# The first row tile in two column halves, one on ScalarE's DMA queue and one on SyncE's

## Chip, cores, metric

One core of a Trainium2 chip. The metric is the device time of one execution in microseconds (us), and medians of several executions are quoted. All runs used here are fast, with a mean granted TensorE clock of 0.64 to 0.67. Engines: PE (matmul), DVE (VectorE), ACT (ScalarE), POOL (GpSimd), SP (SyncE).

## The reference

```python
def reference(a, b):            # a, b: float32, 8 x 2176 x 2176
    prod = np.matmul(a, b)
    return np.diagonal(prod, axis1=1, axis2=2).sum(axis=-1).astype(np.float32)
```

The trace of a product is the sum of a[i,k] b[k,i]. So no matrix product is needed: each element of a and b is read once, multiplied with one partner and added. The inputs are 303 MB.

## The kernel before

For each of eight batches, row tiles of a are loaded, transposed on PE into `at`, and then row tiles of b are multiplied with it and summed, mostly on DVE. GpSimd issues nearly all loads and casts f32 to bf16 in the DMA. Two row groups of 512 rows go together in one load (4352 KB in SBUF), into one of three staging buffers:

```python
    stage = ctx.enter_context(tc.tile_pool(name="stage", bufs=3))
    single = ctx.enter_context(tc.tile_pool(name="single", bufs=3))
    ...
    def load(src, start, m, count):
        ...
        with in_order():
            issued = nc.gpsimd.dma_start(out=part, in_=rows)
```

The very first row tile (128 rows, 1.114 MB) is an exception. SyncE loads it as plain f32 into a staging buffer (`words`), and ACT and DVE cast half of it each:

```python
    def load_first(src, start):
        words = stage.tile([P, DOUBLE * ROWS, N], bf16, tag="stage")
        plain = words.bitcast(f32).rearrange("p r k -> p (r k)")[:, :N]
        half = N // 2
        t = single.tile([P, 1, N], bf16, tag="single")
        nc.sync.dma_start(out=plain, in_=src[start:start + P, :])
        nc.scalar.copy(out=t[:, 0, :half], in_=plain[:, :half])
        nc.vector.tensor_copy(out=t[:, 0, half:], in_=plain[:, half:])
        return [(start, 1, t)]
    ...
            if not tiles:
                groups = load_first(a[bi], start)
                ahead, issued = load(a[bi], *loads[1])
                with tc.issue_after(issued.ins):
                    constants()
            elif ahead is not None:
                groups, ahead = ahead, None
            else:
                groups, _ = load(a[bi], start, m, count)
```

`words` takes one of the three staging buffers, so GpSimd's third large load can be issued only after both casts. The first two large loads take the other buffers.

Of the kernel before, what the change touches and what calls it, by code (L numbers as in the profile page):

```python
# [20 lines left out]
def kernel(  # L21
# [6 lines left out]
    nc = tc.nc  # L28
    P = 128
# [58 lines left out]
    def load_first(src, start):  # L88

        words = stage.tile([P, DOUBLE * ROWS, N], bf16, tag="stage")  # L90
        plain = words.bitcast(f32).rearrange("p r k -> p (r k)")[:, :N]
        half = N // 2
        t = single.tile([P, 1, N], bf16, tag="single")
        nc.sync.dma_start(out=plain, in_=src[start:start + P, :])
        nc.scalar.copy(out=t[:, 0, :half], in_=plain[:, :half])  # L95
        nc.vector.tensor_copy(out=t[:, 0, half:], in_=plain[:, half:])  # L96
        return [(start, 1, t)]
# [119 lines left out]
    for bi in range(BATCH):  # L217
# [8 lines left out]
        for start, m, count in loads:  # L226
# [9 lines that stand above are left out]
            for start, m, a_t in groups:  # L236
                last_transpose = transpose_group(at, a_t, start, m, b_groups)
# [12 lines left out]
        for start, m, count in ([(*g, 1) for g in b_groups] if last else joined(b_groups)):  # L250
            if last and start == N - P:
# [3 lines left out]
                for g0, g1 in LAST_PIECES:  # L255
                    lo, hi = g0 * WIDE, min(g1 * WIDE, N)
                    with in_order():
                        loaded.append(nc.gpsimd.dma_start(  # L258
                            out=row[:, lo:hi], in_=b[bi, start:start + P, lo:hi]
# [3 lines left out]
                for g in range(2, n_wide):  # L263
                    half = ROWS // 2
# [21 lines left out]
            out=tiles["sums"][:, bi:bi + 1], in_=acc[:, :cols], axis=mybir.AxisListType.X  # L286
# [4 lines left out]
    with tc.issue_after(last_transpose.ins):  # L291
        for n, (x, y) in enumerate(pe_work):
            nc.tensor.matmul(  # L293
                trace_ps, x, y, start=(n == 0), stop=(n == len(pe_work) - 1),
            )
    late_acc = tiles["late"]
    for n, (x, y) in enumerate(late):
# [6 lines left out]
        start=True, stop=True,  # L304
    )
    parts = [tiles["sums"][:, BATCH - 1:BATCH]] + [late_acc[:, n:n + 1] for n in range(len(late) + 1)]
    for n, part in enumerate(parts):
        nc.tensor.matmul(  # L308
            total[:, BATCH - 1:BATCH], tiles["ones"], part,
            start=(n == 0), stop=(n == len(parts) - 1),  # L310
# [3 lines left out]
        out=out.rearrange("(a b) -> a b", a=1),  # L314
        in_=tiles["result"][:1, :BATCH],
# [31 lines left out]
```

## Time and profile before

| | before |
|---|---|
| time, median of the first 3 runs (range) | 710.42 us (710.14 to 710.47) |
| span of the profiled execution | 708.7 us |
| read from HBM | 303.04 MB, 428 GB/s over the span |
| first tile: issue, casts start | 0.74, 5.85 us |
| third large load issued | 7.25 us |
| first, second large load in use on PE | 26.40, 47.06 us |

The timeline's lines read: start, duration, engine, line, operation, output<-input, count, and in brackets the idle time before and who ended it. "ACTq" and "SPq" are DMA issues. The lines themselves stand in the prediction.

### The profile page before, as it was taken

What the parts mean: (1) busy time and instruction counts of PE and PEld (TensorE: products, weight loads), DVE (VectorE), ACT (ScalarE), POOL (GpSimd) and SP (SyncE); (2) the same over time, 40 slices, a digit from 0 to 9 for tenths busy, and PEclk for the clock granted to TensorE, in tenths of its full rate; (3) what the DMA queues carried; (4) which work ended last, traced back from release to release, by engine and by line L of the source; (5) the groups of instructions that cost most, each with busy time, mean ns of one, the idle gap of its engine ahead of it and who ended that gap; (6) DMA issues with size and microseconds to landing.
All of it is one profiled execution on the core that took longest, in us unless ns stands there. A gap on an engine that the chain in (4) does not pass through costs nothing.

```text
span 708.7 us, 3573 instructions
## 1 busy us (share of the span) xinstructions
PE 197.8 (28%) x1342; PEld 184.2 (26%) x1342; DVE 420.6 (59%) x455; ACT 196.8 (28%) x210; POOL 35.0 (5%) x61
## 2 busy tenths in 40 slices
PE   1542006420055100551006600056000670006705
PEld 0542005410054100550006500056000560005605
DVE  0223996139952399523994349943499334993396
ACT  2344005430064200652006510066000670006700
POOL 1000000000010000100001000000000000000010
PEclk9977556765577655776557765577655775557765
DMA  9999999999999999999999999999999999999997
GB/s 220 220 220 214 209 221 220 219 210 213 223 219 213 214 218 220 219 211 214 220 220 216 212 216 220 217 214 214 220 220 215 213 217 219 217 216 214 217 215 143
DMA packets 11635, 152.30 MB, mean 215 GB/s; under 512 B 866, under 2 KB 1122, under 8 KB 3298
## 3 DMA queue, kind: packets, MB, share of 16 engines
q0 software_dynamic: 11472, 150.97, 100.1%
q1 hardware_dynamic: 146, 1.11, 0.4%
q8 instruction: 10, 0.16, 0.1%
q14 instruction: 7, 0.06, 0.0%
HBM read 303.04 MB, written 0.00 MB: 428 GB/s over the span
## 4 chain that ended last, share of the span: by engine, by line
DMA 54%; DVE 29%; another core or an unknown queue 10%; PE 3%; issue 2%; ACT 1%; POOL 1%; DVEq 0%; POOLq 0%
DMA t<-in_b_dram 42%; DVE scratch L132 29%; DMA t<-in_a_dram 12%; PE ps L165 2%; ACT at L122 1%; POOL t L83 1%; PE trace_ps L293 0%; DVE acc L132 0%; DVEq L132 0%; PE ps L186 0%; POOL identity masks.py:199 0%; DVE at L120 0%; PE total L308 0%; POOL identity masks.py:197 0%
## 5 line engine op out<-in xcount | busy, mean ns | idle before, releaser
L132 DVE CUSTOM_DVE_ANT_1 scratch<-at,t 128x2048 bf16<-128x2048 bf16 (+1 forms) x159 | 319.6, 2010 | 76.7 <-DMA t<-in_b_dram 69.4
L122 ACT COPY at<-ps 128x1024 bf16<-128x1024 bf16 x208 | 194.5, 1039 | 472.0 <-PE ps L165 472.0
L165 PE MATMUL ps<-identity,t 128*128 128x128 f32 x1071 | 176.8, 332 | 480.5 <-DMA t<-in_a_dram 255.4
L165 PEld LDWEIGHTS ps<-identity,t 128*128 128x128 f32 x1071 | 164.9, 213 | 489.2 <-DVE sums L285 322.0
L120 DVE COPY at<-ps 128x1024 bf16<-128x1024 bf16 (+2 forms) x104 | 93.6, 903 | 201.0 <-PE ps L165 183.7
L83 POOL DMA_DIRECT2D t<-in_a_dram x23 | 15.4, 669 | 357.8 <-DVE acc L132 213.3
L83 POOL DMA_DIRECT2D t<-in_b_dram x27 | 17.0, 632 | 292.8 <-DVE acc L132 145.0
L186 PE MATMUL ps<-identity,t 128*128 128x128 bf16 x170 | 16.4, 219 | 5.3 <-DVE at L120 5.0
L293 PE MATMUL trace_ps<-t,at 128*128 128x128 bf16 x80 | 9.6, 290 | 22.7 <-DMA t<-in_b_dram 22.3
L293 PEld LDWEIGHTS <-at 128*128 128x128 bf16 x89 | 9.8, 122 | 23.6 <-issue 22.9
L186 PEld LDWEIGHTS <-t 128*128 128x128 bf16 x170 | 13.0, 100 | 8.5 <-issue 8.3
L132 DVE DVE_READ_ACCUMULATOR2_ANT acc<- 128x1 f32 x166 | 13.6, 82 | 0.0
L96 DVE CAST t<-words 128x1088 bf16<-128x1088 f32 x1 | 0.7, 727 | 5.0 <-DMA words<-in_a_dram 5.0
L132 DVE CUSTOM_DVE_ANT_1 scratch<-at,b_t 128x256 bf16<-128x256 bf16 (+1 forms) x3 | 1.5, 515 | 1.6 <-DMA b_t<-in_b_dram 1.6
L132 DVE CUSTOM_DVE_ANT_0 scratch<-at,t 128x128 bf16<-128x128 bf16 x7 | 2.0, 291 | 0.2
L95 ACT CAST t<-words 128x1088 bf16<-128x1088 f32 x1 | 1.1, 1098 | 3.8 <-DMA words<-in_a_dram 3.8
L258 POOL DMA_DIRECT2D b_t<-in_b_dram x3 | 1.6, 567 | 0.0
L285 DVE TENSOR_REDUCE sums<-acc 128x1 f32<-128x22 f32 (+1 forms) x8 | 1.4, 174 | 0.3
L95 ACT ACT_TABLE_LOAD x1 | 1.3, 1283 | 0.7 <-PEq L331 0.7
L293 PE MATMUL trace_ps<-b_t,at 128*128 128x128 bf16 x9 | 1.3, 290 | 0.0
L308 PE MATMUL total<-late,ones 128*1 128x1 f32 x8 | 0.5, 163 | 0.3 <-DVE late L132 0.3
masks.py:199 POOL TENSOR_SCALAR_AFFINE_SELECT identity<-identity 128x128 f32<-128x128 f32 (+1 forms) x2 | 0.5, 307 | 0.0
(14 smaller groups left out, 2.4 us busy)
## 6 DMA issues: line engine op xcount, KB each, us to landing
t<-in_a_dram POOLq DMA_DIRECT2D x16, 4352.0 KB, 44.1
t<-in_b_dram POOLq DMA_DIRECT2D x14, 4352.0 KB, 51.8
t<-in_b_dram POOLq DMA_DIRECT2D x3, 2176.0 KB, 32.4
t<-in_b_dram POOLq DMA_DIRECT2D x9, 544.0 KB, 54.8
t<-in_a_dram POOLq DMA_DIRECT2D x7, 544.0 KB, 45.5
words<-in_a_dram SPq DMA_DIRECT2D x1, 1088.0 KB, 5.1
t<-in_b_dram POOLq DMA_DIRECT2D x1, 1088.0 KB, 14.7
b_t<-in_b_dram POOLq DMA_DIRECT2D x1, 256.0 KB, 19.6
```

The lines of the kernel that those rows point to most:

```text
L83: issued = nc.gpsimd.dma_start(out=part, in_=rows)
L95: nc.scalar.copy(out=t[:, 0, :half], in_=plain[:, :half])
L96: nc.vector.tensor_copy(out=t[:, 0, half:], in_=plain[:, half:])
L120: last_copy = nc.vector.tensor_copy(out=dst, in_=src)
L122: nc.scalar.copy(out=dst, in_=src)
L132: nc.vector.tensor_tensor_reduce(out=out, in0=x, in1=y, scale=1.0, scalar=0.0, op0=MUL, op1=ADD, accum_out=acc,)
L165: nc.tensor.transpose(ps[:, n * m + r, :], words[:, r, c0:c0 + step * (P - 1) + 1:step], tiles[f32],)
L186: last_transpose = nc.tensor.transpose(ps16[:, n, r, :], a_t[:, r, c0:c0 + P], tiles[bf16],)
L258: loaded.append(nc.gpsimd.dma_start(out=row[:, lo:hi], in_=b[bi, start:start + P, lo:hi]))
L285: nc.vector.reduce_sum(out=tiles["sums"][:, bi:bi + 1], in_=acc[:, :cols], axis=mybir.AxisListType.X)
L293: nc.tensor.matmul(trace_ps, x, y, start=(n == 0), stop=(n == len(pe_work) - 1),)
L308: nc.tensor.matmul(total[:, BATCH - 1:BATCH], tiles["ones"], part, start=(n == 0), stop=(n == len(parts) - 1),)
```

## The change

Its intent: the two casts belong to two engines and need one half each. If each half is issued by a separate queue, both could be issued at once and ACT could start on its own half without waiting for the other.

```diff
-        nc.sync.dma_start(out=plain, in_=src[start:start + P, :])
+        nc.scalar.dma_start(out=plain[:, :half], in_=src[start:start + P, :half])
+        nc.sync.dma_start(out=plain[:, half:], in_=src[start:start + P, half:])
```

## The prediction

> **What bounds the kernel now**
>
> I read the page from the top: busy shares, the forty slices, the queues. Then the chain of waits, then the timeline of the first ten microseconds, and last the final twenty-five.
>
> Busy shares and slices first. No engine is near full, but the DMA row is full nearly everywhere.
>
> ```profile
> span 708.7 us, 3573 instructions
> PE 197.8 (28%) x1342; PEld 184.2 (26%) x1342; DVE 420.6 (59%) x455; ACT 196.8 (28%) x210; POOL 35.0 (5%) x61
> ...
> DMA  9999999999999999999999999999999999999997
> ...
> q0 software_dynamic: 11472, 150.97, 100.1%
> q1 hardware_dynamic: 146, 1.11, 0.4%
> ...
> HBM read 303.04 MB, written 0.00 MB: 428 GB/s over the span
> ```
>
> The reader is to see three things. The busiest engine (DVE) works 59% of the span. The software queue that GpSimd feeds, casting f32 to bf16 on the way (so 302 MB read become 151 MB written), takes 100% of the sixteen DMA engines' time. The hardware queue, on which the disputed first tile travels, takes 0.4%. So the kernel is bound by moving 303 MB; at 428 GB/s over the span, 1 MB read is worth 2.3 us, and the change neither adds nor removes a byte.
>
> Does the software queue ever run dry, so that an earlier release upstream could buy something? Where it feeds from:
>
> ```profile
> t<-in_a_dram POOLq DMA_DIRECT2D x16, 4352.0 KB, 44.1
> t<-in_b_dram POOLq DMA_DIRECT2D x14, 4352.0 KB, 51.8
> ...
> words<-in_a_dram SPq DMA_DIRECT2D x1, 1088.0 KB, 5.1
> ```
>
> A large load needs about 20.5 us of the engines (4.46 MB written at 217 GB/s; the first two land at 26.4 and 46.9 in the timeline, 20.5 apart), but stands 44 to 52 us between issue and landing. The difference, 23 us or more in the median, is time behind earlier loads. The thinnest place is the end: at 682.64 the loads of the last five row tiles begin to be issued, and the first of these lands 14.7 us later although its 1088 KB need 5.1 us; even there some 9.6 us of work is ahead in the queue.
>
> Now the start, where the change lies (timeline, 0 to 10 us: start, duration, engine, work, idle before it and who ended that):
>
> ```profile
> 0.74 1.28 ACT L95 ACT_TABLE_LOAD   x1 [0.74 <-PEq L331]
> 0.74 0.40 SPq L94 DMA_DIRECT2D words<-in_a_dram  x1
> 1.25 0.82 POOL L83 DMA_DIRECT2D t<-in_a_dram  x1 [0.80 <-POOLq L331]
> 2.93 0.72 POOL L83 DMA_DIRECT2D t<-in_a_dram  x1
> 5.85 1.10 ACT L95 CAST t<-words 128x1088 bf16<-128x1088 f32 x1 [3.83 <-DMA words<-in_a_dram]
> 5.85 0.73 DVE L96 CAST t<-words 128x1088 bf16<-128x1088 f32 x1 [4.98 <-DMA words<-in_a_dram]
> 7.06 1.58 PEld L165 LDWEIGHTS ps<-identity,t 128*128 128x128 f32 x8 [7.06 <-issue]
> 7.25 0.72 POOL L83 DMA_DIRECT2D t<-in_b_dram  x1 [3.60 <-ACT t L95]
> ...
> 26.40 6.39 PEld L165 LDWEIGHTS ps<-identity,t 128*128 128x128 f32 x32 [17.62 <-DMA t<-in_a_dram]
> ...
> 37.97 1.28 POOL L83 DMA_DIRECT2D t<-in_b_dram  x2 [30.00 <-PE ps L186]
> ...
> 47.03 6.32 PEld L165 LDWEIGHTS ps<-identity,t 128*128 128x128 f32 x32 [9.54 <-issue]
> ```
>
> The first tile is issued at 0.74 and lands at 5.85; its casts, eight transposes and copies are over by about 10.2, after which PE, ACT and DVE sit idle until the first large load lands at 26.40. Only one DMA issue hangs on the first tile: the one at 7.25, which waits for the casts because the tile's raw words borrow a staging buffer. But two large loads are then ahead of it, the second landing about 47. The release could be about 39 us later before the engines ran dry.
>
> The chain of waits agrees: it starts with GpSimd's preamble and steps onto the second large load of a (issued 2.93, 44.00 us); the first tile is not in it. I read its start with care: that load waits behind the first load, so its own issue time sets nothing either.
>
> **What the Trainium skill says**
>
> DMA: Bandwidth & Descriptors, "Issuing engines are not separate DMA queues": DMAs started by different engines run on the same 16 DMA engines and interleave, and issuing from several "will only save the time on the sequencer it takes to initiate the DMA". Here that issue is 0.40 us of SyncE, an engine with nothing else to do.
>
> The same page, "Queues, rings and completion order": each DMA engine goes round its rings packet by packet. So the two halves will share the engines with each other, and later with the software queue; that they differ in landing by little is my inference.
>
> The same page, "Anatomy of one DMA": a fit for software DMAs of about 2.0 us plus bytes over 436 GB/s. For 1.114 MB this is 4.6 us; the trace has 5.1 for this hardware DMA. Roughly agreeing, and as a split it says that half the bytes, alone, would land 1.3 us sooner, but two halves together would not.
>
> ScalarE: Activation LUTs, "What ACT_TABLE_LOAD costs": 1283 ns for the load. The trace has exactly 1283 ns. It matters since the new ScalarE issue stands before it.
>
> **The change part by part**
>
> Removed: one SyncE DMA of 128 rows of 8704 B. Added: a ScalarE DMA and a SyncE DMA, each 128 rows of 4352 B. Compared instruction by instruction, PE, DVE and GpSimd keep the same order; ScalarE gains the one issue ahead of its table load; ScalarE's cast waits for ScalarE's half only and DVE's for SyncE's half.
>
> 1. Bytes: 1.114 MB before and after: 0 us.
>
> 2. Issue on ScalarE: one more instruction of about 0.40 us (SyncE's row). The table load moves from 0.74 to about 1.2 and ends about 2.5 instead of 2.02. ScalarE then idles until 5.85 (3.83 us of wait in its row), so 0.45 is swallowed: 0 us.
>
> 3. Descriptors: 128 more data packets and 16 more completions (146 packets were 128 rows, 16 completions and 2 for the output). In all 11,635 becomes about 11,779. Even if each cost the engine as much as 20 ns more (my allowance, not measured), 9 more per engine are 0.2 us: between 0 and +0.2 us, the only term that is surely in the DMA engines' time.
>
> 4. Start of the stream: narrow slices of the trace show no bytes before 1.7 us, 139 GB/s from 1.5 to 2.5 and some 400 from 3.0. Two issuers might fill this ramp sooner. The ramp is under-filled by about two thirds for about 1 us; saving half is 0.3 us. It is off the engines' time only if GpSimd's first load (issued 1.25, landing at 26.40) moves up with it. Between -0.4 and 0 us.
>
> 5. Landing of the halves: both at about 5.1 us from issue (4.6 to 5.9). If one is 0.5 us earlier, its cast starts earlier, but the transposes interleave both and need the later one. PE's start moves by perhaps -0.5 to +0.7 from 7.06, the release at 7.25 likewise; against some 39 us of slack: 0 us.
>
> 6. The rest of the program, 10 to 709 us: same instructions, same loads: 0 us. The tail after the last bytes is untouched.
>
> Sum: -0.4 to +0.2 us, centre -0.1, that is 0.01% of 710. I predict 710.4.
>
> **The rivals**
>
> First: starting earlier pays. If everything downstream hung on the first tile, a half landing after 2.6 instead of 5.1 us would give up to 2.5 us, 707.9. For it: the four engines do wait on it at 5.85 to 7.25. Against it: they all wait again at 26.40 for a load whose time is set by the DMA engines. And the halves contend with each other, so no such landing is likely.
>
> Second: contention. With two hardware rings, one half could fall behind the software queue, whose packets are larger (150.97 MB in 11,472 packets, 13 KB written and 26 KB read each on average). An engine needs some 1 us for one at its share of 428 GB/s, so a half could land 1 to 3 us later. The bytes moved meanwhile are bytes of the large loads, so these land sooner by the same amount and the end stays: 710.4. This rival changes the early picture, not the time.
>
> Third: a change of rate later on, since a shift of the start changes how the sixteen engines and the bursts of DVE and PE lie against each other. The slices vary between 209 and 223 GB/s. This could go either way; a fifth of a percent is 1.4 us: 709.0 to 711.8. Against it: three runs of the kernel before lie within 0.33 us, so the stream does not seem sensitive to small shifts.
>
> **Range and chances**
>
> The sum gives 710.0 to 710.6. I widen it for the third rival and for a new run on the chip, where 0.2% is 1.4 us; 8 in 10 that it lies in 709.2 to 711.6. Faster by over 2% would need 14 us, many times the whole life of the first tile's load; slower by 2% would need a stall of the same size that no part of the change can make. One in a hundred each.
>
> **What would show it**
>
> Step 1 and 3: 303 MB read again, hardware packets near 290 over two queues, software queue near 100%. Step 2: the table load about 0.45 later and the wait after it shorter by as much. Step 4 and 5: the halves land 4.6 to 5.9 us after issue, PE starts between 6.5 and 7.8, GpSimd's third load is issued between 6.7 and 8.0. Step 6: the first large load lands within 0.5 us of 26.40, the second within 0.5 of 46.93, and all later landings move by the same fraction of a microsecond.
>
> It would be wrong if the software queue showed a hole in the slices, if the landing at 26.40 moved by more than 1 us and the end moved with it, or if the mean rate over the span left 428 GB/s by more than 0.3%.

## The result, and the profile after

The changed kernel takes 710.49 us (710.28 to 710.56, 6 runs) and the kernel before 710.50 (710.14 to 710.84, 6 runs). The ratio is 0.9999, with a 95% interval of 0.9986 to 1.0012. A ratio is the mean time of one kernel's fast runs over the mean of the other's of the same rounds, so it is not quite the ratio of the medians quoted. A repeat (e7 below) gave 1.0000 (0.9988 to 1.0013). It is the same time, as predicted.

Packets, queues and the total read on the page of the changed kernel:

```profile
span 708.7 us, 3576 instructions
...
DMA packets 11779, 152.30 MB, mean 215 GB/s; under 512 B 882, under 2 KB 1138, under 8 KB 3570
...
q0 software_dynamic: 11472, 150.97, 100.2%
q10 hardware_dynamic: 144, 0.56, 0.2%
q1 hardware_dynamic: 146, 0.56, 0.2%
...
HBM read 303.04 MB, written 0.00 MB: 428 GB/s over the span
```

The reader is to see the hardware queue's 1.11 MB in two equal parts, 144 more packets in all (128 rows and 16 completions), and nothing else moved: the same bytes at the same mean rate, and the software queue still fills the engines.

The timeline of the changed kernel, at the same places as the prediction shows of the kernel before:

```profile
0.74 0.40 SPq L95 DMA_DIRECT2D words<-in_a_dram  x1
0.74 0.38 ACTq L94 DMA_DIRECT2D words<-in_a_dram  x1
...
1.16 1.28 ACT L96 ACT_TABLE_LOAD   x1 [1.16 <-PEq L332]
...
5.73 1.10 ACT L96 CAST t<-words 128x1088 bf16<-128x1088 f32 x1 [3.29 <-DMA words<-in_a_dram]
5.92 0.73 DVE L97 CAST t<-words 128x1088 bf16<-128x1088 f32 x1 [5.05 <-DMA words<-in_a_dram]
...
7.18 0.72 POOL L83 DMA_DIRECT2D t<-in_b_dram  x1 [3.53 <-ACT t L96]
```

Both queues issue at 0.74. The table load slides from 0.74 to 1.16, and ACT's wait shrinks from 3.83 to 3.29. The halves land within 0.2 us of each other, one 0.12 us before and one 0.07 us after the whole tile did. The third load is issued 0.07 us sooner.

One thing did not go by the prediction. The first two large loads were in use at 27.47 and 48.16 instead of 26.40 and 47.06 (PE's rows of the timeline):

```profile
27.47 5.96 PE L166 MATMUL ps<-identity,t 128*128 128x128 f32 x32 [18.44 <-DMA t<-in_a_dram]
...
48.16 5.86 PE L166 MATMUL ps<-identity,t 128*128 128x128 f32 x32 [10.02 <-DMA t<-in_a_dram]
```

Each large load has sixteen reports in the raw trace, one for each DMA engine, and PE starts after the last of them. These are the sixteen reports of the first large load, sorted, read from the raw trace (its clock runs some 0.2 us ahead of the timeline's):

```
before        26.09 26.29 26.30 26.32 26.33 26.36 26.37 26.38 26.38 26.42 26.48 26.51 26.53 26.56 26.58 26.60
changed       26.33 26.34 26.34 26.37 26.40 26.40 26.45 26.50 26.52 26.55 26.58 26.60 26.63 26.63 26.70 27.67
changed (e7)  26.14 26.17 26.18 26.29 26.29 26.31 26.35 26.36 26.36 26.39 26.40 26.42 26.47 26.49 26.53 26.60
```

Fifteen of sixteen engines are within 0.3 us of where they were, and one came a microsecond late. In the second run of the same kernel there is no such straggler.

### The profile page after: what moved, and what is told of

It reads as the page before. It is cut to its first block, busy times and chain, and to the rows that moved or that the text cites. A ratio compares the mean times of both kernels' runs of the same rounds, so it can differ in the third digit from the quotient of the medians.

```text
span 708.7 us, 3576 instructions
## 1 busy us (share of the span) xinstructions
PE 197.2 (28%) x1342; PEld 183.5 (26%) x1342; DVE 420.5 (59%) x455; ACT 196.7 (28%) x210; POOL 35.0 (5%) x61
## 2 busy tenths in 40 slices
DMA packets 11779, 152.30 MB, mean 215 GB/s; under 512 B 882, under 2 KB 1138, under 8 KB 3570
## 4 chain that ended last, share of the span: by engine, by line
DMA 54%; DVE 30%; another core or an unknown queue 9%; PE 2%; issue 2%; ACT 1%; POOL 1%; DVEq 0%; POOLq 0%
DMA t<-in_b_dram 42%; DVE scratch L133 29%; DMA t<-in_a_dram 13%; PE ps L166 2%; ACT at L123 1%; DVE at L121 1%; POOL t L83 1%; PE trace_ps L294 0%; DVE acc L133 0%; PE ps L187 0%; DVEq L133 0%; POOL identity masks.py:199 0%; PE total L309 0%; POOL identity masks.py:197 0%
```

## The experiments

The main theory: the end is set by the bytes that sixteen DMA engines have to move, the software queue is never empty, and the first tile hangs on nothing that the end waits for until its release is some 39 us late. The rivals: the first tile is on the path; the two queues contend and delay it; the early shift changes the rate later.

| run | time, us (runs) | before in the same rounds | ratio (95%) |
|---|---|---|---|
| e1, kernel before again | 710.51 (5) | 710.65 | 0.9998 (0.9985 to 1.0011) |
| e2, both halves on SyncE | 710.45 (5) | 710.65 | 0.9997 (0.9984 to 1.0009) |
| e3, casts held to 27 us | 710.40 (5) | 710.65 | 0.9999 (0.9985 to 1.0013) |
| e4, casts held to 48 us | 715.68 (5) | 710.65 | 1.0073 (1.0060 to 1.0085) |
| e5, tile fetched four times | 718.98 (4) | 710.42 | 1.0120 (1.0105 to 1.0136) |
| e6, tile last, by GpSimd | 711.44 (5) | 710.42 | 1.0014 (1.0002 to 1.0027) |
| e7, changed kernel again | 710.41 (5) | 710.42 | 1.0000 (0.9988 to 1.0013) |
| e8, extra copies: one ring, whole rows | 718.46 (4) | 710.50 | 1.0111 (1.0096 to 1.0126) |
| e9, extra copies: two rings, whole rows | 718.90 (4) | 710.50 | 1.0116 (1.0101 to 1.0131) |
| e10, extra copies: one ring, half rows | 722.55 (4) | 710.50 | 1.0169 (1.0152 to 1.0186) |

All ten gave correct results.

**e1 and e7, what chance does.** e1 is the kernel before without an edit, e7 the changed kernel without one.

> The kernel before, once more, as a kernel of its own: what two identical programs differ by. All theories: ratio 1.000 within 0.2%. For the landing of the first large load: the kernel before had its last of sixteen completions at 26.6 us (15 of them by 26.6), the changed one had fifteen by 26.7 and one at 27.7. If such a straggler is chance, this run shows landings anywhere between 26.4 and 27.7; if it is made by the halves, this run shows 26.4 again (within 0.3).

> The changed kernel once more. Time: ratio 0.998 to 1.002. What is asked is the one late completion of sixteen in the first large load (27.7 us against 26.7 for the others) that only the changed kernel's profile has shown, and neither the one-queue halves nor the held one. If it is chance, it is absent here (all sixteen within 26.0 to 26.8); if the change makes it, it is there again, about 1 us late, and still without effect on the end.

Identical programs differ by 0.02% in the ratio, with an interval of 0.13% either way, so nothing under about 0.9 us can be told from time alone. The straggler was absent in both (last report at 26.72 and 26.60), as it was in e2, e3 and e4. For e1 alone either reading would do; e7, and e3 and e4, which issue the halves as the changed kernel does, show that the halves do not make it every time. The raw trace names no engine for a packet, but it has one that fits: a packet of the software queue that started at 5.37 us took 2.49 us, against 1.30 in the median and at most 1.54 in the profiles of before, e1, e2, e3 and e7. Why it took so long stays open. It did no harm: the third load's sixteen reports end at 68.80 in the changed kernel and at 68.69 before.

(In that third load each of e1, e2, e3, e6 and e7, like the two first profiles, has its last report 0.8 to 1.0 us behind most of the others. The trace has one 16 KB instruction fetch of about 0.97 us within that load. One run speaks for this as the cause: in e10 the fetch came at 54.74, before the third load's first packet at 57.37, and there the last two of the sixteen reports are 0.05 us apart. No edit tested it.)

**e2, both halves on one queue.**

```diff
-        nc.scalar.dma_start(out=plain[:, :half], in_=src[start:start + P, :half])
+        nc.sync.dma_start(out=plain[:, :half], in_=src[start:start + P, :half])
```

> Both halves on SyncE's queue, one after the other: the same descriptors as the change, but one ring. Theory (one set of DMA engines, bytes decide): time 710.4 (ratio 0.998 to 1.002); the first half lands early, about 3.9 us after the start of its issue (5.1 less the 1.3 us that 0.56 MB take at 428 GB/s), so ScalarE's cast starts near 4.7 instead of 5.7; the second half lands about 5.2 to 5.6 us after the first issue. Rival (halves always share, wherever they are issued): both land at 5.0 to 5.5 after the first issue. Rival (the early picture matters): an earlier cast would shorten the end by up to 1 us.

The timeline of e2, the two issues, the two casts and PE's start:

```profile
0.74 0.38 SPq L94 DMA_DIRECT2D words<-in_a_dram  x1
1.18 0.42 SPq L95 DMA_DIRECT2D words<-in_a_dram  x1
...
4.54 1.10 ACT L96 CAST t<-words 128x1088 bf16<-128x1088 f32 x1 [2.52 <-DMA words<-in_a_dram]
...
5.79 1.98 PE L166 MATMUL ps<-identity,t 128*128 128x128 f32 x8 [5.79 <-ACT t L96]
...
5.86 0.73 DVE L97 CAST t<-words 128x1088 bf16<-128x1088 f32 x1 [4.99 <-DMA words<-in_a_dram]
```

In one queue the halves come home one after the other, 1.32 us apart, which is what 0.557 MB take at 428 GB/s (1.30 us). ACT's half is there at 4.54 instead of 5.73, and PE starts at 5.79 instead of 6.97. Issued through two queues, which was meant to bring ACT's half sooner, both halves came home only when the bytes of both had been moved. The rival "halves always share" falls. (The second half came 5.1 us after the first issue, a little before the 5.2 to 5.6 expected.) The time is unchanged even so: 1.2 us of earlier transposes buy nothing.

**e3 and e4, how late may the first tile be used?** Both casts are held until a large load has landed: each engine first copies half of that load into the cast's output, and the cast then overwrites it. In e3 it is the first load, in e4 the second.

```diff
+        def cast(big):
+            nc.scalar.copy(out=t[:, 0, :half], in_=big[:, 0, :half])
+            nc.vector.tensor_copy(out=t[:, 0, half:], in_=big[:, 0, half:])
             nc.scalar.copy(out=t[:, 0, :half], in_=plain[:, :half])
             nc.vector.tensor_copy(out=t[:, 0, half:], in_=plain[:, half:])
 ... (called once the first load, in e4 also the second, is issued)
```

> The changed kernel with both casts of the first tile held until the first large load has landed (each engine first copies a half of that load into the cast's output, which is then overwritten): the first tile is used some 21 us later and GpSimd's third load is released near 29.5 instead of 7.2. Theory (slack of some 39 us, the queue is full until about 47): time unchanged, 710.4, ratio 0.998 to 1.002, although the first transposes start near 29 instead of 7. Rival (first tile on the path): about +21 us, 731.

> The same, held until the second large load has landed: release of the third load near 49.5, after the queue has run dry at about 46.5. Theory: a hole in the DMA from about 46.5 until some 2.3 us after the issue at 49.5 (the delay between the first GpSimd issue at 1.25 and its first bytes, an estimate), so +3 to +6 us: 713.5 to 716.5, ratio 1.004 to 1.009, once, and nothing for the 42 us by which the tile is later. Rival (first tile on the path): about +42 us, 752. Rival (slack larger than I think): unchanged.

GpSimd's third load in the timelines of e3 and of e4:

```profile
28.96 0.72 POOL L83 DMA_DIRECT2D t<-in_b_dram  x1 [25.32 <-ACT t L100]
```

```profile
49.59 0.71 POOL L83 DMA_DIRECT2D t<-in_b_dram  x1 [45.94 <-ACT t L100]
```

Stretches of 2 us of e4 (columns: stretch, length, busy time of PE, PEld, DVE, ACT and POOL, granted clock, DMA share, GB/s):

```profile
44.00:46.00 2.00, 0.00 (x0) 0.00 (x0) 0.00 (x0) 0.00 (x0) 0.00 (x0) 1.00 0.73 157
46.00:48.00 2.00, 0.00 (x0) 0.00 (x0) 0.90 (x2) 0.94 (x1) 0.00 (x0) 1.00 0.01 0
48.00:50.00 2.00, 0.56 (x3) 0.60 (x4) 0.27 (x1) 1.26 (x2) 0.41 (x1) 1.00 0.00 0
50.00:52.00 2.00, 2.00 (x12) 1.94 (x11) 0.23 (x1) 1.43 (x2) 0.30 (x1) 1.00 1.00 139
```

In e3 the release comes 21.8 us later than in the changed kernel and the time stays (a ratio of 0.9999). In e4 it comes 42.4 us later and the kernel is 5.0 us longer, no more than an eighth of the delay. The raw trace accounts for it: the second large load's last packet ends at 46.70 and the next load's first starts at 51.02, a hole of 4.3 us, and the first sixteen packets after the hole took 2.0 us each in the mean against 1.30 later, 0.7 more. So the slack is real and ends where it was said to end, when the second large load has landed and nothing stands behind it. Its length was not measured by steps. An estimate: packets started 1.4 us after the issue (49.59 to 51.02), so a release at about 45.3 would still have been in time, which is 38 us later than in the changed kernel. The prediction's 39 left out these 1.4 us.

**e5, is a byte of the first tile worth what the bandwidth says?** The tile is fetched four times. Three copies go into spare room of `words` and nobody uses them.

```diff
+        for n in (1, 2, 3):
+            lo = n * N
+            nc.scalar.dma_start(out=spare[:, lo:lo + half], in_=src[start:start + P, :half])
+            nc.sync.dma_start(out=spare[:, lo + half:lo + N], in_=src[start:start + P, half:])
```

> The changed kernel with the first tile fetched four times, both halves on both queues, three of the copies into spare room of the same staging buffer, used by nobody: 3.34 MB more read. Theory (bytes decide the end): +3.34 MB over 428 GB/s = +7.8 us, 718.4 (716.5 to 720), ratio 1.009 to 1.013, and GpSimd's third load released near 15, far before about 55 when the queue would be dry, so no hole. Rival (hardware-queue bytes are hidden beside the software queue, since that is held by something else): unchanged, below 712. The wanted halves are first in their rings and should still land near 5 to 6 after issue.

The time grew by 8.6 us for 3.34 MB (718.98 less 710.42). The theory said 7.8 and the rival zero, so bytes on the hardware queues are not hidden; they take their place in the same sum. But my picture of when they land was wrong. GpSimd's third load, which has to wait for the copies, went out at 47.00 and not near 15:

```profile
47.00 2.00 POOL L83 DMA_DIRECT2D t<-in_b_dram  x3 [43.36 <-DMA words<-in_a_dram]
```

From 14 to 26 us, on all sixteen engines together, the raw trace has 121 packets of the software queue of 17,408 B (1.30 us each in the median), 118 of SyncE's and 116 of ACT's queue (4352 B, 0.18 and 0.17 us; 27 of these 234 are completion reports of 4 B). The three queues are served nearly packet for packet, whatever the packets' sizes. A queue's packets on one engine are called a ring here. Per engine the copies are 24 packets in each ring; at 1.3 + 2 x 0.16 = 1.6 us a turn that is an estimate of 39 us after the first halves; the last copy's reports ended at 46.35, 40 us after them. This was found afterwards, so it needed a test of its own.

**e8, e9, e10, the turns.** The same three spare copies in other packings; the edit is in the body of the loop alone. They were run on another chip.

```diff
 e8:   nc.sync.dma_start(out=spare[:, lo:lo + N], in_=src[start:start + P, :])
 e9:   copy 1 like this on nc.scalar, copy 2 on nc.sync, copy 3 half of the partitions on each
 e10:  as e5, but both halves on nc.sync
```

> The four copies again, but the three spare copies as whole rows of 8704 B, all on SyncE's queue (24 packets for each DMA engine in one ring). New theory from the four copies: once the software queue has packets, each engine serves one packet of each ring in turn; a software packet takes about 1.3 us, one of 4352 B about 0.16, so 24 turns of 1.3 + 2 x 0.16 = 1.6 us brought the last copy home near 46. Here a turn is 1.3 + 0.32 = 1.6 us and there are again 24: release of GpSimd's third load again near 44 to 48; time again 718 to 720. Rival (one hardware ring gets half as much of the engines as two): release near 60 or later. Rival (engines share by bytes, half and half): release near 20.

> The same three spare copies as whole rows, one and a half on each of the two queues: 12 packets of 8704 B for each engine in each ring. Turn theory: 12 turns of 1.3 + 2 x 0.32 = 1.9 us = 23 us after about 6, release near 28 to 31; time unchanged against the other copies, 718 to 720, since the bytes are the same. Rival (it is the bytes that wait, however they are packed): release near 47 as with the halves.

> The same three spare copies as half rows of 4352 B, all on SyncE's queue: 48 packets for each engine in one ring. Turn theory: 48 turns of 1.3 + 0.16 = 1.46 us would be 70 us, so about 33 of them are done when the software queue runs dry near 54; the other 15 then go alone in about 2.5 us, release near 56 to 60, and a hole of some 3 to 5 us in the software queue: 722 to 725. Rival (the number of packets does not matter): release near 47 and 719.

The release of the third load in the timelines of e8, e9 and e10:

```profile
46.39 2.00 POOL L83 DMA_DIRECT2D t<-in_b_dram  x3 [42.74 <-ACT at L127]
```

```profile
31.81 0.72 POOL L83 DMA_DIRECT2D t<-in_b_dram  x1 [28.15 <-DMA words<-in_a_dram]
```

```profile
55.96 2.00 POOL L83 DMA_DIRECT2D t<-in_b_dram  x3 [52.32 <-ACT at L128]
```

| | packets per engine and ring | release expected | release measured | time |
|---|---|---|---|---|
| e5: two rings, half rows | 24 | 15 (wrong, before the turns) | 47.0 | 718.98 |
| e8: one ring, whole rows | 24 | 44 to 48 | 46.4 | 718.46 |
| e9: two rings, whole rows | 12 | 28 to 31 | 31.8 | 718.90 |
| e10: one ring, half rows | 48 | 56 to 60 | 56.0 | 722.55 |

(In e8 and e10 the bracket names ACT, not the DMA, as the one that ended the wait; brackets are put down by inference. ACT's last work on `words`, its cast, had ended at 6.9 and 7.0. The raw trace has the copies' last report at 45.83 in e8 and 55.40 in e10, 0.56 us before the issue, much as in e5, at 46.35, 0.65 before. So the copies are what the load waited for.) e9's release is 0.8 us above its range. Time to landing goes with the number of packets in a ring, not with the bytes. With whole rows, the second ring brought the same 3.34 MB home 15 us earlier; cut into halves over two rings it brought nothing over whole rows in one. The end does not care (718.5 to 719.0) as long as the software queue stays fed. e10 exceeds that: the software queue's last packet ends at 52.9 and its next starts at 57.4, and e10 pays 3.6 us more than e5. The copies themselves fill the hole until 55.1. That leaves 2.3 us, and 0.7 for slow first packets as in e4: 3.0 of the 3.6, by estimate.

**e6, no early tile at all.** The first tile goes through GpSimd's queue behind both large loads, cast in the DMA like all others.

```diff
-                groups = load_first(a[bi], start)
-                ahead, issued = load(a[bi], *loads[1])
+                first, issued = load(a[bi], *loads[1])
                 with tc.issue_after(issued.ins):
                     constants()
+                second, _ = load(a[bi], *loads[2])
+                groups, _ = load(a[bi], start, 1, 1)
+                ahead = [first, second]
```

> The first tile loaded by GpSimd's queue, cast on the way like all others, behind the two large loads, so no hardware load and no casts: it lands near 47 to 49 instead of 5.8. Theory: the same bytes read and the queue never dry (first large load landing near 24, first buffer released near 60 while the third large load lasts until about 67): 710.4, perhaps up to 1.5 us more because GpSimd's first bytes start later than SyncE's did (issue at 1.25 against 0.74, and packets of the first load seen only from about 4.9), so 710 to 712, ratio 0.999 to 1.003. Rival (an early first tile is worth what it brings forward): +40 us.

The first transposes start at 48.01 us instead of 7.09 and the kernel is 1.0 us longer (711.44 against 710.42), not 40. Where that microsecond lies, in half-microsecond stretches, first of before and then of e6:

```profile
1.50:2.00 0.50, 0.00 (x0) 0.00 (x0) 0.00 (x0) 0.50 (x1) 0.50 (x1) 1.00 0.99 139
2.00:2.50 0.50, 0.00 (x0) 0.00 (x0) 0.00 (x0) 0.02 (x1) 0.49 (x4) 1.00 0.53 139
2.50:3.00 0.50, 0.00 (x0) 0.00 (x0) 0.00 (x0) 0.00 (x0) 0.50 (x3) 1.00 0.58 244
```

```profile
2.00:2.50 0.50, 0.00 (x0) 0.00 (x0) 0.00 (x0) 0.01 (x1) 0.49 (x4) 1.00 0.00 0
2.50:3.00 0.50, 0.00 (x0) 0.00 (x0) 0.00 (x0) 0.00 (x0) 0.50 (x3) 1.00 2.62 348
```

Without SyncE's load the first packet starts at 2.77 us instead of 1.76 (raw trace), and the tile and both large loads are all home at 47.87 instead of 46.93: the microsecond is lost by then. So the early hardware load does earn something, about 1 us, but by starting the DMA engines sooner and not by starting PE sooner, since e3, with PE 22 us later, lost nothing. The changed kernel keeps that, and adds nothing: its three stretches from 1.5 to 3.0 us have 87, 70 and 305 GB/s, 231 KB in all against 261 KB before.

## Why the prediction was right

- The sum, -0.1 us: too small for these runs to tell from zero. What was right is the argument that nothing the change moves reaches the end.
- Bound and step 1 (bytes): shown. The read total and the rate are unchanged, and e5 shows that added hardware bytes are paid for: 8.6 us for 3.34 MB, 2.6 us per MB where the prediction's rate gives 2.3 (2.4 in e8). The 0.8 us that e5 took beyond this rate was not traced.
- Step 2 (issue on ScalarE): shown. The issue took 0.38 us, the table load moved by 0.42, and ACT's wait took it up.
- Step 3 (packets): the count of 11,779 was exact. Their cost, 0 to 0.2 us, is below what the run times resolve. The packets' own times give an estimate: 168 ns in the median for half a row and 328 for a whole one, so two halves cost 8 ns more, 0.06 us for the 8 rows of each engine.
- Step 4 (ramp): the saving of up to 0.4 us did not come. The first stretches hold no more bytes than before (231 KB against 261, and 222 in e7), so this term is zero as far as can be seen.
- Step 5 (halves): both landed 5.0 and 5.1 us after issue; PE started 0.12 us sooner and the third load 0.07. That halves contend was an inference then; e2 shows it, by the same halves landing 1.32 us apart in one queue. One reading in this step was wrong: that the transposes interleave both halves and need the later one. In e2 PE started at 5.79, before DVE's cast of the second half at 5.86; four of the eight transposes ran on ACT's half alone. Nothing hung on it, since an earlier PE buys nothing.
- Step 6 (the rest): right in the sum, but one of the signs that the prediction named for it failed. The first two large loads were to stay within 0.5 us and moved by 1.07 and 1.10. The step took the landing of a load for the state of the stream, while it is the slowest of sixteen engines; in e7 it did not recur. The prediction had named as fatal a landing that moved by more than 1 us and took the end with it; the first half of that came true, and the end did not follow.
- The slack of 39 us: shown to lie between 22 and 42 by e3 and e4, and put at 38 by the estimate above.
- First rival (early start pays): refuted by e2, e3 and e6. Second rival (contention): absent in the change, as the halves landed where the whole tile had. The raw trace shows why: 245 of their 256 packets had started when the software queue's first did, at 5.0 us, so the two hardly met. The runs e5, e8, e9 and e10 show that the mechanism is real, and my allowance of 1 to 3 us was far too small for data that meets the software queue's stream: the first spare copy of e5, cut into halves like the tile, landed at 19.1, 13 us after the tile, and all three took 40. The allowance also used the average packet of 13 KB and 1 us; the large loads' packets are 17,408 B and 1.30 us. Third rival (rate): nothing beyond 0.13%.

## What to carry to other kernels

When one resource is full from start to end, ask of an earlier arrival only whether that resource starts sooner or ever runs dry; here the first tile could be used 22 us later for nothing, and 42 us later for the price of the hole alone. To get half of a small transfer early, issue both halves in one queue in the order of need: that brought the first half at 4.54 us, where two queues brought both at 5.7 to 5.9. And beside a queue of large packets, a transfer's delay follows the number of packets that it has in each ring, so use long rows, and a second ring for more turns, if that delay matters at all.

## What the Trainium skill lacked or had wrong

- DMA: Bandwidth & Descriptors, "Issuing engines are not separate DMA queues", says that issuing from several engines will only save issue time: true for the end (718.46 against 718.90 us), but not for a landing. Against a running software queue, the same 3.34 MB in whole rows allowed the next load at 31.8 us from two rings and at 46.4 from one.
- The same page, "Queues, rings and completion order", has the turns by packet, and these runs agree: 121, 118 and 116 packets of three queues in the same 12 us. It lacks what follows from unequal packets: 17,408 B of the software queue to 4352 or 8704 B of a hardware ring per turn, so that 48 packets in a ring (e10) were not home until 55.40, when two large loads of some 20 us each had ended at 53.35.
- The same page, "Anatomy of one DMA": its fit, made for DMAs that GpSimd issues, gives an estimate of 4.6 us for 1.114 MB and 3.3 for half. For SyncE's the trace has 5.1 and, for the first half in front of the other, 3.8: each 0.5 us more. The difference of the two, 1.3 us, agrees. The page has no fit for SyncE's and ACT's queues.
- No page that I read says that an engine which reports with the others in one execution may report a microsecond behind them in the next (27.67 against 26.70 for the fifteenth), so that a load's landing in a single profile can move by 1 us without any change of rate.
- No page that I read has the slow first packets of a software queue that starts while the engines are idle: 15 of the first 16 took 1.7 to 2.3 us in each of e4, e6 and e10, against 1.30 in the stream.
